# A decoder trunk on one core: the attention weight's piece emitted behind the step's Strassen operand

## The chip, the cores and the metric

The kernel runs on one core of one Trainium2 chip. The metric is the device time of one execution in microseconds; the time of a kernel is the median of several runs. Three runs of the kernel before are at hand, and one further execution was taken with the profiler.

## The reference

The reference is a trunk of two layers over 512 tokens of width 1024, in float32. Layer 0 mixes by causal pooling, layer 1 by stick-breaking attention with 16 heads of 64. Each layer ends in a squared-ReLU MLP of inner width 4096. The shared key and value projection stands between the layers.

```python
def sq_relu_mlp(h, w_up, w_down):
    u = jnp.matmul(h, w_up)
    return jnp.matmul(jnp.square(jax.nn.relu(u)), w_down)

def reference(x, ...):
    for layer in range(DEPTH):
        h = rms_norm(x, mix_pre_g[layer])
        m = pool_mixer(...) if layer < N_A else (stick_breaking_attention(q, k, v) @ w_o)
        x = x + rms_norm(m, mix_post_g[layer])
        h = rms_norm(x, mlp_pre_g[layer])
        x = x + rms_norm(sq_relu_mlp(h, w_up[layer], w_down[layer]), mlp_post_g[layer])
        if layer == N_A - 1:
            kv = jnp.matmul(rms_norm(x, kv_norm_g), w_kv)
    return x
```

## The kernel before

**Numbers in two parts.** Every matrix product is made of float32 values that are split into a high part, rounded to the fast matmul type (fp32r), and a low part, the difference. One product then takes three matmuls: high by high, high by low, low by high. A split is a copy on ScalarE and a subtraction on VectorE: L192 and L194 for the weights that are loaded raw and split at once (`weight`), L314 and L315 for everything that `split` handles.

**The first MLP** (`mlp` with l = 0) has 32 blocks of the up projection, 128 inner columns each, named by j. An up block is 24 matmuls (`up_block`, L766 to L770). ScalarE then takes ReLU and square (L675, L676). The down projection of the first 28 blocks is done in five groups of 2, 3, 3, 3 and 3 pairs of blocks, each by Strassen's scheme (the class `Seven`): seven products in place of eight, each with an operand `a` made of squares (`left`, additions on VectorE at L595) and an operand `w` made of down weights (`right`, L614). Both are split. `make(i)` makes the operands of product i; `product` (L640) runs its matmuls, 18 for a group of three pairs, and adds two halves of the result to y (L649, in part L646). The raw down weights come in two large loads a group, `load(0)` and `load(1)` (L579), in the tiles w1 and xn3. The last four blocks, 28 to 31, are not done by Strassen: their four down weights (dn28 to dn31) are loaded and split at the end of the stage, and `finish` runs their matmuls (L333 to L335).

**One step** of the stage is product i of group g. In code it is: the product, then the call that splits a piece of an attention weight, then the next up block, then the operands of product i + 2 (of the next group at the end of a group), then `fill`, which asks for the next weight in the queue. Steps count from 0 to 34 over the five groups; steps 1 to 33 have a piece.

**Pieces.** Thirty attention weights of 128 x 1024 (key, query, value and output) are prepared during this stage, so that attention need not split them: `split_apart` at L230. Each passes through four calls in a row: it is loaded (L245) into one of five buffers (three with the tag "apart", the spare tile, the tile of the gain row); it is scaled on ScalarE, column group by column group (L204; eight instructions for a key or query, four for a value, none for an output weight); its high part is copied into one half of the tile wx (L254) and the low part is made in place (L255); both parts are stored to device memory (L235, tensors "kept"). Every call does one of these for each of up to four pieces. Later, `make` at L265 brings the two parts back as they are ("w<-kept"). The first piece is loaded in step 1, the last in step 30 and stored in step 33.

**What orders the work.** Outside the stages that name a manual order, the order of each engine's instructions is worked out at build time by a scheduler with modelled durations (`schedule_with_timeline_sim=True`); where several instructions are ready, the one emitted first goes first. `tc.issue_after(x)` ties what is emitted within it to run behind x on x's engine. Around `split_apart` stand two of them, with the last split on ScalarE and on VectorE (`latest`). The weight copies of the up blocks are tied in the same way to `behind`, which is brought up to `latest` ahead of each fill. DMAs all go out on SyncE's queue in one order.

**Buffers at the end of the stage.** Tiles with the same tag share buffers, and a new tile waits for the last use of the old one. In step 33 the code takes tiles for the four down weights out of buffers that the stage no longer needs: dn30's raw weight and its high part get two of the three "apart" buffers, those of the last pieces but two and but one; dn31's raw weight gets a buffer of the Strassen operand a, that of product 5 of the last group. The fourth value weight that attention wants (v03 here) comes back into the tile wx, which the high parts of the pieces used. In the queue of weights, the four first value weights stand ahead of the four down weights.

Of the kernel before, what the change touches and what calls it, by code (L numbers as in the profile page):

```python
# [36 lines left out]
def halves(x, n=1):  # L37
    return x.rearrange("p (h a b) -> p h a b", h=n, a=2)


def unwoven(x, n=1):
    return x.rearrange("p (h b a) -> p h a b", h=n, a=2)
# [83 lines left out]
def trunk(ctx, tc, x, bands, grow, pw, wup, wdn, wq, wk, wv, wo, out):  # L126
# [12 lines left out]
    def name(s):  # L139
        uid[0] += 1  # L140
        return f"{s}{uid[0]}"

    def ps():
        return psum.tile([P, 512], F32, tag="ps", name=name("ps"))
# [19 lines left out]
    def spare_tile():  # L164
        return work.tile([P, D], F32, tag="spare", name=name("spare"))
# [10 lines left out]
    behind, latest = {}, {}  # L176
# [53 lines left out]
    def split_apart(mp):  # L230
        if going and going[0] is not None and going[0][1] == 3:
            k, _, raw, hi, _ = going.pop(0)
            kept[k] = dram.tile([2, P, D], F32, tag=f"kept{len(kept)}", name=name("kept"))
            for n, t in enumerate((hi.bitcast(F32), raw)):
                latest["sp"] = nc.sync.dma_start(kept[k][n], t)  # L235
        if apart:
            k, src, scaled = apart.pop(0)
            n = len(apart) % 5
            if n < 3:
                raw = mp.tile([P, D], F32, tag="apart", bufs=3, name=name("apart"))  # L240
            else:
                raw = spare_tile() if n == 3 else work.tile([P, D], F32, tag="grow", name=name("apart"))

            with tc.issue_after(latest["sp"].ins) if "sp" in latest else nullcontext():
                nc.sync.dma_start(raw, src)  # L245
            going.append([k, 0, raw, None, scaled])
        for x in going:
            k, n, raw, hi, scaled = x
            if n == 1:
                if scaled is not None:  # L250
                    scaled(raw)
            elif n == 2:
                hi = x[3] = apart_hi[0][:, len(kept) % 2]
                nc.scalar.copy(hi, raw)  # L254
                nc.vector.tensor_tensor(out=raw, in0=raw, in1=hi.bitcast(F32), op=ALU.subtract)  # L255
            x[1] += 1
# [19 lines left out]
    def get(key):  # L276
        while key not in made:
            make()
        return made.pop(key)
# [265 lines left out]
    def y_tiles():  # L545
        return [work.tile([P, D], F32, tag=f"y{t}", name=name(f"y{t}")) for t in range(T)]
# [104 lines left out]
    def mlp(l, mp, update):  # L651

        gate[0] = False
        y = y_tiles()
        firsts = [2 * sum(GROUPS[:g]) for g in range(len(GROUPS))]
        plain = 2 * sum(GROUPS)
        groups = [Seven(l, firsts[g], n, mp) for g, n in enumerate(GROUPS)]

        steps = [n for n in range(1, 34)] if l == 0 else []
        squares = []  # L660
        written = {None}

        def up(j, pu=None):
            if pu is None:
                pu = ps()
                up_block(pu, get(("up", l, j)), slice(0, S))
                n = 1
            else:
                n = 2
            if j < plain:  # L670
                g = max(g for g, f in enumerate(firsts) if f <= j)
                r = groups[g].part(j - firsts[g])
            else:
                r = mp.tile([P, S], F32, tag="rp", name=name("rp"))
            nc.scalar.activation(halves(r, n), unwoven(pu, n), ACT.Relu)  # L675
            nc.scalar.activation(r, r, ACT.Square)  # L676
            if j >= plain:
                if j < plain + 3:
                    if j == plain:
                        squares.append(mp.tile([P, 3, 2, S], F32R, tag="r", bufs=2, name=name("sq")))  # L680
                    a = squares[0][:, j - plain]
                else:
                    a = work.tile([P, 2, S], F32R, tag="spare", name=name("sq"))
                split(r, a[:, 0], a[:, 1])
                squares.append((a[:, 0], a[:, 1]))

        entering = dict(normed_by)
        groups[0].load(0)
        groups[0].squares()
        if l == 0:  # L690
            apart_hi[0] = wts.tile([P, 2, D], F32R, tag="wx", name=name("wx"))
        need(0, 1)
        n0 = 2 * GROUPS[0]
        first = early[:]
        while len(first) < n0:
            first.append((ps(), get(("up", l, len(first)))))
        for j, (pu, w) in enumerate(first):
            if j == n0 - 1:
                need(2, 3)
                groups[0].load(1)  # L700
            if j >= len(early):
                up_block(pu, w, slice(0, S // 2))
        early.clear()
        for j, (pu, w) in enumerate(first):
            up_block(pu, w, slice(S // 2, S))
            up(j, pu)
            fill()

        with tc.issue_after(latest["act"].ins), tc.issue_after(latest["dve"].ins):
            for i in range(2):  # L710
                groups[0].make(i)
        for g, group in enumerate(groups):
            coming = groups[g + 1] if g + 1 < len(groups) else None
            if coming:
                coming.squares()
            ups = list(range(firsts[g + 1], firsts[g + 1] + 2 * GROUPS[g + 1]) if coming else range(plain, NJ))
            if g == 0:
                up(ups.pop(0))
                fill()
            else:  # L720
                with tc.issue_after(latest["dve"].ins):
                    while entering:
                        entering.popitem()[1].homogeneous_eps()
            for i in range(7):
                group.product(i, y, written if g == 0 else None)
                if 7 * g + i in steps:
                    with tc.issue_after(latest["act"].ins), tc.issue_after(latest["dve"].ins):
                        split_apart(mp)
                if ups:
                    up(ups.pop(0))  # L730
                if i + 2 < 7:
                    group.make(i + 2)
                    if i + 2 == 4 and coming:
                        coming.load(0)
                    if i + 2 == 6 and coming:
                        coming.load(1)
                elif coming:
                    coming.make(i + 2 - 7)
                elif i == 5:
                    piece = lambda tag, k, bufs=1: mp.tile([P, k, D], F32R, tag=tag, bufs=bufs, name=name("dn"))  # L740
                    w, e, x = piece("w1", 3), piece("e", 1), piece("w", 3, 2)
                    c = piece("apart", 1, 3)[:, 0]
                    dn_raw["dn", l, NJ - 2] = mp.tile([P, D], F32, tag="apart", bufs=3, name=name("dn"))
                    dn_raw["dn", l, NJ - 1] = mp.tile([P, D], F32, tag="a", bufs=2, name=name("dn"))
                    dn_pool[0] = [[w[:, 0], w[:, 1]], [w[:, 2], e[:, 0]], [c, x[:, 2]], [x[:, 0], x[:, 1]]]

                if l == 0:
                    behind.update(latest)
                fill(1 + (coming is None and i == 6))
        assert not apart and not going  # L750
        gpost = gain_row((R_MLP_POST0, R_MLP_POST1)[l])
        count[0] = 0
        w = [get(("dn", l, j)) for j in range(plain, NJ)]
        dn_pool[0] = None
        fill(ahead)
        finish(l, squares[1:], w, y, lambda t, y: update(t, y, gpost))
# [21 lines left out]
    with tc.tile_pool(name="mix0", bufs=1, reuse_waits="tile") as mp:  # L778
# [138 lines left out]
        def half_up(j):  # L917
# [3 lines left out]
        steps = {  # L921
            "j": lambda n: nc.gpsimd.tensor_copy(eye, wpool[n][:, D:]),
            "z": busy, "r": scale_row, "e": scale_copy, "w": linear, "q": first_squares, "v": first_norm,
            "b": own_band, "p": pooled, "c": copied, "f": reached, "m": mixed,
            "s": lambda t, h: ups[t].squares_of(h, left["m", t, h]),
            "g": lambda t, h: ups[t].product(h, left["m", t, h]),
            "X": lambda t: (ups[t].first_total(nc.vector), ups[t].first_rstd()),
            "Y": lambda t: (ups[t].second_total(nc.vector), ups[t].rstd()),
            "V": lambda t: ups[t].first_rstd(), "a": lambda t, h: ups[t].add_part(h),
# [490 lines left out]
```

## Time and profile before

| | |
|---|---|
| median of 3 runs | 905.44 us (904.74 to 905.92) |
| profiled execution | 904.5 us |
| its span, first to last instruction | 902.7 us |
| granted TensorE clock, mean | 0.999 |
| bytes moved by DMA | 155.73 MB |
| the first MLP's steps in the trace | about 60 to 324 us |

The profile names engines PE (TensorE's matmuls), PEld (its weight loads, beside them), DVE (VectorE), ACT (ScalarE), POOL (GpSimd) and SP (SyncE, whose queue issues the DMAs: SPq). "out<-in" are the program's tile names with the buffer numbers left out; L254 is line 254 of the kernel before. A row of a timeline has start, length, engine, line, operation, tiles, shapes and a count; in brackets stands the idle time ahead of it and what ended that. The length of an issue row is the time to issue; the time to landing comes from the view of the DMAs. In the chain of waits each row is a start, a length and what the end of the program waited for at that time.

### The profile page before, as it was taken

The page shows a single profiled execution, that of the slowest core. Times are in us where ns is not written, and L with a number is a line of the kernel's source. Part 1 is how long each engine was busy: PE and PEld are TensorE (multiplying, and loading weights), DVE is VectorE, ACT ScalarE, POOL GpSimd, SP SyncE. Part 2 cuts the span into 40 slices and gives each one's busy share as a digit, 9 for nine tenths or more (in the row PEclk, how much of TensorE's full clock was granted, in tenths as well). Part 3 has the DMA queues.
Part 4 walks back from the last instruction along what each step waited for, and adds up shares of the span by engine and source line. Part 5 has one row for each costly group of instructions (what it writes and reads, how often), then busy time and mean ns, then how long its engine had stood idle before and what let it go on. Part 6 is the DMA issues. An engine that isn't in the chain of part 4 may idle for free.

```text
span 902.7 us, 12343 instructions
## 1 busy us (share of the span) xinstructions
PE 890.8 (99%) x4688; PEld 786.0 (87%) x4688; DVE 692.7 (77%) x797; ACT 557.3 (62%) x986; POOL 40.9 (5%) x85
## 2 busy tenths in 40 slices
PE   9999999999999999999999999999999999999997
PEld 7998888888888878888999888898888888888886
DVE  5876798998978977268777489885696976957866
ACT  6668979888784747256555474875545454544632
POOL 3200000000000004000000001200000000000002
PEclk9999999999999999999999999999999999999999
DMA  8444969789697770643152371342504233133002
GB/s 306 142 147 150 358 219 367 305 277 401 223 343 263 269 273 2 216 157 140 57 189 82 109 288 47 141 163 77 203 26 162 94 140 117 47 140 117 23 24 94
DMA packets 42973, 155.73 MB, mean 173 GB/s; under 512 B 4257, under 2 KB 4385, under 8 KB 42914
## 3 DMA queue, kind: packets, MB, share of 16 engines
q1 hardware_dynamic: 42914, 154.95, 47.8%
q8 instruction: 37, 0.61, 0.3%
q14 instruction: 22, 0.18, 0.1%
HBM read 121.38 MB, written 33.55 MB: 172 GB/s over the span
## 4 chain that ended last, share of the span: by engine, by line
PE 84%; DVE 5%; DMA 4%; ACT 4%; issue 2%; POOL 1%; SPq 0%; POOLq 0%; ACTq 0%; DVEq 0%
PE ps L640 24%; PE ps L769 14%; PE ps L766 14%; PE ps L770 14%; PE ps L334 4%; PE ps L335 4%; PE ps L333 4%; PE ps L1105 2%; PE ps L1124 2%; PE ps L1149 2%; DMA xn<-in_wdn 1%; PE ps L440 1%; DMA apart<-in_wk 1%; PE ps L894 1%; ACT xn L318 1%
## 5 line engine op out<-in xcount | busy, mean ns | idle before, releaser
L640 PE MATMUL ps<-w,a 128*128 128x512 f32 x1176 | 265.9, 379 | 0.4 <-ACT a L314 0.4
L769 PE MATMUL ps<-xnh,w 128*128 128x512 f32 (+1 forms) x704 | 253.4, 362 | 0.0
L770 PE MATMUL ps<-xnl,w 128*128 128x512 f32 (+1 forms) x704 | 252.8, 360 | 0.0
L766 PE MATMUL ps<-xnh,w 128*128 128x512 f32 (+1 forms) x704 | 252.3, 360 | 0.3 <-DVE w L915 0.3
L640 PEld LDWEIGHTS ps<-w,a 128*128 128x128 f32 x1176 | 222.0, 189 | 32.7 <-ACT a L314 0.8
L766 PEld LDWEIGHTS ps<-xnh,w 128*128 128x128 f32 x704 | 132.9, 190 | 16.0 <-DVE w L915 0.4
L770 PEld LDWEIGHTS ps<-xnl,w 128*128 128x128 f32 x704 | 133.5, 190 | 15.2
L769 PEld LDWEIGHTS ps<-xnh,w 128*128 128x128 f32 x704 | 133.0, 190 | 15.4
L194 DVE TENSOR_TENSOR w<-raw,w 128x1024 fp32r<-128x1024 f32 x58 | 70.8, 1221 | 46.9 <-ACT w L192 46.9
L649 DVE TENSOR_TENSOR y<-ps,y 128x512 f32<-128x512 f32 x124 | 84.0, 686 | 25.7 <-PE ps L640 25.2
L192 ACT CAST w<-raw 128x1024 fp32r<-128x1024 f32 x58 | 60.6, 1045 | 64.1 <-PE ps L766 62.6
L314 ACT CAST a<-r 128x768 fp32r<-128x768 f32 (+1 forms) x60 | 47.4, 789 | 62.3 <-PE ps L640 40.9
L315 DVE TENSOR_TENSOR a<-r,a 128x768 fp32r<-128x768 f32 (+1 forms) x60 | 54.0, 899 | 10.8 <-ACT a L314 10.8
L314 ACT CAST w<-e 128x1536 fp32r<-128x1536 f32 (+1 forms) x30 | 41.7, 1391 | 32.1 <-DVE e L614 23.9
L1086 DVE TENSOR_TENSOR_SCAN e<-u,begin 128x1280 f32<-128x1280 f32 x16 | 45.2, 2825 | 18.6 <-ACT u L1070 17.9
L315 DVE TENSOR_TENSOR w<-e,w 128x1536 fp32r<-128x1536 f32 (+1 forms) x30 | 49.4, 1646 | 0.7 <-ACT w L314 0.5
L204 ACT ACTIVATE apart<-apart,eye 128x128 f32<-128x128 f32 (+1 forms) x132 | 43.0, 404 | 0.2 <-DMA apart<-in_wk 0.2
L315 DVE TENSOR_TENSOR w<-xn,w 128x1536 fp32r<-128x1536 f32 (+1 forms) x20 | 33.0, 1649 | 4.5 <-ACT w L314 4.1
L675 ACT ACTIVATE r<-ps 128x512 f32<-128x512 f32 x56 | 33.0, 589 | 5.4 <-PE ps L766 5.4
L676 ACT ACTIVATE r<-r 128x512 f32<-128x512 f32 x56 | 35.3, 631 | 1.3
L315 DVE TENSOR_TENSOR w<-w,w 128x1536 fp32r<-128x1536 f32 (+1 forms) x20 | 33.0, 1648 | 3.5 <-ACT w L314 3.5
L322 POOL TENSOR_SCALAR stat<-stat,eps 128x1 f32<-128x1 f32 x8 | 5.4, 680 | 604.9 <-ACT xn L318 604.9
(140 smaller groups left out, 1322.1 us busy)
## 6 DMA issues: line engine op xcount, KB each, us to landing
raw<-in_wup SPq DMA_DIRECT2D x64, 512.0 KB, 4.5
w<-kept SPq DMA_DIRECT2D x60, 512.0 KB, 4.3
kept<-wx SPq DMA_DIRECT2D x30, 512.0 KB, 5.6
w<-in_wdn SPq DMA_DIRECT2D x8, 1536.0 KB, 7.0
kept<-apart SPq DMA_DIRECT2D x24, 512.0 KB, 6.2
xn<-in_wdn SPq DMA_DIRECT2D x8, 1536.0 KB, 8.2
apart<-in_wk SPq DMA_DIRECT2D x7, 512.0 KB, 8.0
apart<-in_wq SPq DMA_DIRECT2D x7, 512.0 KB, 9.6
```

Of the source, the lines that this page charges most:

```text
L192: nc.scalar.copy(hi, raw)
L194: nc.vector.tensor_tensor(out=lo, in0=raw, in1=hi.bitcast(F32), op=ALU.subtract)
L204: nc.scalar.mul(c, c, gc[:, at : at + 1])
L314: latest["act"] = nc.scalar.copy(hi, src)
L315: latest["dve"] = nc.vector.tensor_tensor(out=lo, in0=src, in1=hi.bitcast(F32), op=ALU.subtract)
L333: nc.tensor.matmul(dst, ah, bh, start=start, stop=False)
L640: nc.tensor.matmul(bank, a[:, x, q, TS[t]], woven(w[:, z, q], NS[0]), start=start and q == 0 and k == 0, stop=q == self.n - 1 and k == 2, ...
L649: nc.vector.tensor_tensor(out=part, in0=bank, in1=part, op=ALU.add)
L766: nc.tensor.matmul(pu[:, cols], wl[:, k, :], moving(xnh, k), start=False, stop=k == KC - 1)
L769: nc.tensor.matmul(pu[:, cols], wh[:, k, :], moving(xnh, k), start=k == 0, stop=False)
L770: nc.tensor.matmul(pu[:, cols], wh[:, k, :], moving(xnl, k), start=False, stop=False)
L1086: nc.vector.tensor_tensor_scan(out=self.e[:, ::-1], data0=self.u[:, 1:][:, ::-1], data1=begin[:, ::-1], initial=0.0, op0=ALU.mult, op1=ALU ...
```

## The change

The call of `split_apart`, with its two `issue_after`, moves within the step: from ahead of the step's up block and operands to behind them. It stands ahead of `behind.update(latest)` and `fill` as before. What a call does is unchanged, and so are the steps that have one. As `latest` now holds the splits of the step's own operands, the piece's instructions on ScalarE and VectorE are tied to run behind those; before they were tied behind the operands of the step before. In step 33 the call comes behind the lines that take the tiles for the down weights.

```diff
             for i in range(7):
                 group.product(i, y, written if g == 0 else None)
-                if 7 * g + i in steps:
-                    with tc.issue_after(latest["act"].ins), tc.issue_after(latest["dve"].ins):
-                        split_apart(mp)
                 if ups:
                     up(ups.pop(0))
                 if i + 2 < 7:
                     group.make(i + 2)
...
                     dn_pool[0] = [[w[:, 0], w[:, 1]], [w[:, 2], e[:, 0]], [c, x[:, 2]], [x[:, 0], x[:, 1]]]
 
+                if 7 * g + i in steps:
+                    with tc.issue_after(latest["act"].ins), tc.issue_after(latest["dve"].ins):
+                        split_apart(mp)
                 if l == 0:
                     behind.update(latest)
                 fill(1 + (coming is None and i == 6))
```

## The prediction

> **What bounds the kernel now.** First the page's head and its busy lines.
>
> ```profile
> span 902.7 us, 12343 instructions
> PE 890.8 (99%) x4688; PEld 786.0 (87%) x4688; DVE 692.7 (77%) x797; ACT 557.3 (62%) x986; POOL 40.9 (5%) x85
> ```
>
> TensorE is busy in 99% of the span. What matters is how much of the missing 1% lies where the change acts. The waits of TensorE alone answer that; the columns are total us, times, longest.
>
> ```profile
> PE ps L334 <- DVE dn L194: 0.8, 1, 0.8
> PE ps L333 <- ACT dn L192: 0.5, 1, 0.5
> PE ps L640 <- ACT a L314: 0.4, 1, 0.4
> ```
>
> These three are all that TensorE waits in the first MLP. Cut into stretches, the stage looks like this (columns: length, then busy us of PE, PEld, DVE, ACT, POOL, the granted clock, DMA share, GB/s):
>
> ```profile
> 109.00:172.00 63.00, 63.00 (x293) 55.02 (x292) 58.62 (x66) 53.74 (x98) 0.00 (x0) 1.00 0.83 308
> 172.00:230.00 58.00, 57.56 (x268) 50.21 (x267) 54.08 (x53) 49.81 (x88) 0.00 (x0) 1.00 0.81 300
> 324.50:349.00 24.50, 23.25 (x110) 19.68 (x109) 17.52 (x24) 12.24 (x29) 5.99 (x10) 1.00 0.33 120
> ```
>
> The second row is short of its length by 0.44 us (the L640 wait, near 172 us), the third by 1.25 us (the two dn waits). So the stage can give back 0.44 + 1.25 = 1.69 us and no more, which is 0.19% of 905.44. The clock is 1.00 throughout. The first row shows where a loss could come from: VectorE is busy 58.62 of 63 us, with 4.4 us of slack.
>
> Is a busy TensorE at its pace? In the chain, one step of a three-pair group runs from one product to the next:
>
> ```profile
> 307.63 3.88 PE ps L640 x18
> 316.69 7.78 PE ps L640 x36
> ```
>
> The 18 matmuls of the first line and the 24 of the up block behind it take 316.69 - 307.63 = 9.06 us, 0.216 us each, and 18 x 0.216 = 3.88 fits the same pace. The change alters no matmul, so this pace stays.
>
> **What the change moves.** Each piece passes through four calls, one a step: load, scaling (L204), high part and subtraction (L254, L255), two stores. In code the call moves behind the up block and the operands of the same step. Where does it stand on ScalarE now? At the start and at the end of the stage:
>
> ```profile
> 80.04 1.04 ACT L314 CAST w<-w 128x1024 fp32r<-128x1024 f32 x1
> 80.98 1.05 ACT L254 CAST wx<-apart 128x1024 fp32r<-128x1024 f32 x1
> ...
> 312.29 1.47 ACT L314 CAST w<-xn 128x1536 fp32r<-128x1536 f32 x1
> 313.66 1.04 ACT L254 CAST wx<-apart 128x1024 fp32r<-128x1024 f32 x1
> ...
> 321.35 1.47 ACT L314 CAST w<-xn 128x1536 fp32r<-128x1536 f32 x1
> 322.72 1.99 ACT L192 CAST dn<-raw 128x1024 fp32r<-128x1024 f32 x2
> ```
>
> The operand w<-w at 80.04 is product 4's, made in step 2; the first L254 belongs to step 3's call (load in 1, scale in 2, split in 3). The last L254 belongs to step 32 and stands behind product 5's operand, made in step 31. So each piece already runs right behind an operand split, that of the step before, because ScalarE has nothing else while the up block runs. issue_after ties it now to the last split of the step before; afterwards to this step's own. The whole chain of pieces thus slides by one step, about 9.06 us, and nearly every slot behind an operand stays filled, by the piece one earlier.
>
> **Middle steps.** Two rows price a piece, eight scalings on ScalarE and a subtraction on VectorE:
>
> ```profile
> 105.40 2.44 ACT L204 ACTIVATE apart<-apart,eye 128x128 f32<-128x128 f32 x8
> ...
> L255 DVE TENSOR_TENSOR apart<-apart,wx 128x1024 f32<-128x1024 f32 x24 | 29.2, 1218 | 0.6 <-ACT wx L254 0.6
> ```
>
> Same instructions, same places behind operands: 0 us. What can still differ is the turn between a piece and the weight copy L192 of the same step, since a piece is now emitted ahead of that step's fill. That puts up to 1.05 + 2.44 us of ScalarE (L254 and eight L204) ahead of a copy whose block is two steps of 9 us away: covered. If that cover fails at the one place where an operand was late, the bound is one piece's subtraction (L255) more, against the whole wait less: between -0.44 and +1.22 us. I take 0, because the work per step is unchanged. [...] DMA order with the big wdn loads also stays: the store of a piece is already issued when its split is done, not when its call is emitted.
>
> **The end of the stage.** Here one step later is not neutral, because the four down weights come next. The chain of waits there:
>
> ```profile
> 324.49 7.14 DMA dn<-in_wdn
> 331.73 1.05 ACT dn L192
> 332.81 1.24 DVE dn L194
> 334.09 0.48 PE ps L334
> ```
>
> The last raw weight (dn31) takes the buffer of product 5's operand a, so its load starts when that product ends, at 324.49. It lands 7.14 us later, and split it ends TensorE's 1.25 us wait. The SyncE queue around it, then the time to landing of three of these transfers:
>
> ```profile
> 312.22 0.49 SPq L235 DMA_DIRECT2D kept<-apart  x1
> 314.73 0.32 SPq L235 DMA_DIRECT2D kept<-wx  x1
> 316.72 0.88 SPq L265 DMA_DIRECT2D w<-kept  x2
> 321.95 0.80 SPq L265 DMA_DIRECT2D w<-kept  x2
> 322.80 0.43 SPq L235 DMA_DIRECT2D kept<-apart  x1
> 324.49 0.33 SPq L182 DMA_DIRECT2D dn<-in_wdn  x1
> ...
> kept<-apart SPq DMA_DIRECT2D x1, 512.0 KB, 8.5
> ...
> kept<-wx SPq DMA_DIRECT2D x1, 512.0 KB, 7.1
> ...
> dn<-in_wdn SPq DMA_DIRECT2D x1, 512.0 KB, 3.7
> ```
>
> The pair at 321.95 brings the fourth value weight (v03) back. It goes into the wx buffer, so it waits for the last kept<-wx: 314.73 + 7.1 = 321.8. It is in flight when dn31 is issued, and so is the last kept<-apart.
>
> VectorE's rows for the last pieces and for dn30:
>
> ```profile
> 316.28 1.22 DVE L255 TENSOR_TENSOR apart<-apart,wx 128x1024 f32<-128x1024 f32 x1
> ...
> 323.16 1.75 DVE L315 TENSOR_TENSOR w<-xn,w 128x1536 fp32r<-128x1536 f32 x1
> ...
> 327.70 1.22 DVE L194 TENSOR_TENSOR dn<-dn,dn 128x1024 fp32r<-128x1024 f32 x1
> ```
>
> After the change the last L254 comes behind product 6's split, at 322.72, and ends near 323.8; the last kept<-wx goes out then. Its landing, 323.8 + 7.1 = 330.9, releases v03's loads. They fall behind dn31 instead of ahead of it. The last subtraction follows the split's own, which ends at 324.9, so the raw store goes out near 326.1. Of three transfers of 0.5 MB issued in the 2.5 us ahead of dn31, one is left. Two fewer are 1.05 MB, at the rate of that stretch
>
> ```profile
> 327.00:331.70 4.70, 4.70 (x23) 4.12 (x22) 2.52 (x3) 0.00 (x0) 0.00 (x0) 1.00 1.03 416
> ```
>
> an estimated 2.5 us. dn31 would land after 4.6 us, between the 3.7 of its sister and the 7.14, and the wait of 1.25 us would go.
>
> What is late next is the third down weight (dn30). Its raw goes into a buffer of the pieces, freed by the store of piece 28 of 30, and its high part into the buffer of piece 29. Piece 28's store moves to the place of piece 29's (312.22, landing after 8.5): 320.7. A load of 3.7 to 7.1 us ends at 324.4 to 327.8, and with 1.05 and 1.24 us of split it is ready at 326.7 to 330.1. TensorE wants its low part here:
>
> ```profile
> 329.82 0.38 PE L334 MATMUL ps<-dn,sq 128*128 128x512 f32 x1
> ```
>
> So 0 to 0.3 us late; if instead piece 29's store, going out between 317.5 (the end of the subtraction at 316.28) and 320.7, takes 8.5 us, the high part starts at 329.2 and the low part ends at 331.6, 1.8 us late. A wait there replaces dn31's rather than adds to it, as 12 matmuls (2.6 us) lie between the two. The subtraction of the last piece also pushes the splits of dn28 to dn30 on VectorE by 1.2 us, and dn30's now ends at 327.70 + 1.22 = 328.92, 0.9 us ahead of the row above: 0.3 us late again.
>
> The end's wait is thus 0 to 1.8 us in place of 1.25: -1.25 to +0.55. I take 0.85 left, -0.4, as dn30's row is nearer to in time than late. v03 itself, landing near 338, is not wanted before the projection that begins here:
>
> ```profile
> 352.57 0.38 PE L333 MATMUL ps<-w,xnh 128*128 128x512 f32 x1
> ```
>
> **Sum.** 0 - 0.4 = -0.4 us. The profiled execution took 904.5 us, 902.7 of span and 1.8 around it: 904.1. That execution lies 0.9 under the median of the runs, 905.44, so against that 905.0. Bounds of the terms: -1.69 to +1.77, 903.7 to 907.2.
>
> **Rivals.** (a) *Slower: SyncE stands still ahead of dn31.* SyncE takes its queue in order, and v03 already held it from 317.6 to 321.95 with a finished store behind. If dn31's load is queued behind the raw store of the last piece it starts at about 326.1, +1.6 us; if behind v03's loads, at 330.9, +6.4 us, giving 906.1 or 910.9 on the profile's scale (907.0 and 911.8 against the median). It decides at one point: whether the last kept<-wx lands before product 5 ends. 323.8 against 324.49 leaves no time for a transfer of 7.1, so the schedule, which is made with modelled durations, should put dn31 first: 0.10.
>
> (b) *Both waits go.* 1.69 us less, 902.8 on the profile's scale, 903.8 against the median. It needs dn30 in time and VectorE's order near 172 to turn out better: 0.10.
>
> (c) *Nothing moves.* If pieces stayed behind the operands that they follow now, the time is 905.4. issue_after forbids it for all but the last calls: 0.10.
>
> (d) *VectorE's tight stretch breaks.* The schedule of the stage is worked out anew, and TensorE's own order with it. One or two operands late by one subtraction each: +1.2 to +2.4, so 906.7 to 907.9. For it: 58.62 of 63 us busy, and one wait of 0.44 there already. Against: an unchanged load per step. 0.08.
>
> [...]
>
> **How the numbers follow.** The forecast, a shift by one step and an end that is worth a few tenths, gets 0.60; its own range is 903.8 to 906.0. What a measurement of this kernel can tell from no change is about 0.2%, 1.81 us. The forecast and (c) lie inside it; of (b) 0.04 may be measured as faster, with (e) 0.06. Of (a) the longer hold, 0.07, and of (d) 0.05 are slower: 0.12. That leaves 0.82 for no change. The range 903.5 to 907.4 takes in the bounds of the terms, (b), (c) and the lesser halves of (a) and (d).
>
> **What would show it.** Right: the first L254 near 88 behind w<-xn, the last near 322.7 behind the last w<-xn; w<-kept of v03 issued near 331, after dn<-in_wdn at about 324.5; dn<-in_wdn landing in 4 to 6 us; the dn waits of TensorE at 0 to 1 us; rows of the middle stretches as before. Wrong: an L254 still at 313.7; dn<-in_wdn issued after 326; TensorE waits at L640 of over 1 us between 100 and 300; a span below 901 without any change in the three waits.

## The result and the profile after

The kernel after took 908.69 us (906.21 to 912.30, 14 runs) beside 904.46 for the kernel before on the same chip (14 runs): a ratio of 1.0047, 95% interval 1.0036 to 1.0058. It is slower by 4.2 us, more than twice what the prediction called no change. Its profiled execution took 907.5 us, with 905.7 of span, 3.0 more than before.

The shift by one step is there as forecast. First ScalarE at the end of the stage, then SyncE's queue with the issue rows of the same stretch:

```profile
321.88 1.47 ACT L314 CAST w<-xn 128x1536 fp32r<-128x1536 f32 x1
323.26 1.04 ACT L254 CAST wx<-apart 128x1024 fp32r<-128x1024 f32 x1
```

```profile
312.14 0.32 SPq L235 DMA_DIRECT2D kept<-apart  x1
318.29 0.33 SPq L182 DMA_DIRECT2D dn<-in_wdn  x1
318.72 0.38 SPq L235 DMA_DIRECT2D kept<-wx  x1
319.19 1.80 SPq L265 DMA_DIRECT2D w<-kept  x2
321.09 0.67 SPq L235 DMA_DIRECT2D kept<-apart  x1
...
325.02 0.62 SPq L182 DMA_DIRECT2D dn<-in_wdn  x1
...
331.38 0.80 SPq L265 DMA_DIRECT2D w<-kept  x2
```

The last L254 stands behind the last operand (forecast 322.7), and v03's pair goes out at 331.38, behind dn31's load at 325.02 (forecast 331 and 324.5). The time went elsewhere. TensorE's waits in the stage, and the two rows at the end (the bracket is the idle time ahead of the row):

```profile
PE ps L333 <- ACT dn L192: 1.2, 1, 1.2
PE ps L640 <- ACT a L314: 1.2, 1, 1.2
PE ps L334 <- DVE dn L194: 0.8, 1, 0.8
```

```profile
331.53 0.48 PE L333 MATMUL ps<-dn,sq 128*128 128x512 f32 x1 [1.22 <-ACT dn L192]
332.79 0.48 PE L334 MATMUL ps<-dn,sq 128*128 128x512 f32 x1 [0.78 <-DVE dn L194]
...
334.14 0.63 PE L333 MATMUL ps<-dn,sq 128*128 128x512 f32 x1
334.57 0.63 PE L334 MATMUL ps<-dn,sq 128*128 128x512 f32 x1
335.00 0.63 PE L335 MATMUL ps<-dn,sq 128*128 128x512 f32 x1
```

The dn waits are 2.00 us, and they now belong to dn30, one block earlier than the dn31 waits of before. Behind them the matmuls start 0.43 us apart instead of 0.216. The stretches say why; the third column from the right is the granted clock:

```profile
324.50:349.00 24.50, 22.50 (x97) 18.62 (x96) 17.98 (x24) 11.33 (x24) 3.71 (x6) 0.93 0.51 191
...
334.00:335.00 1.00, 1.00 (x4) 0.72 (x4) 1.00 (x1) 0.00 (x0) 0.00 (x0) 0.50 1.06 414
335.00:336.00 1.00, 1.00 (x4) 0.81 (x3) 0.07 (x1) 0.00 (x0) 0.00 (x0) 0.50 0.95 311
336.00:338.00 2.00, 2.00 (x8) 1.64 (x7) 0.19 (x1) 0.00 (x0) 0.00 (x0) 0.70 0.93 354
```

From 333.8 to 337.2 the clock is 0.50: eight matmuls at 0.43 instead of 0.216 us, 1.7 us that no busy share shows, since TensorE has 3.42 of 3.42 us busy there.

The L640 wait stands where the second group ends and the third begins. VectorE there, before and then after:

```profile
162.60 0.68 DVE L649 TENSOR_TENSOR y<-ps,y 128x512 f32<-128x512 f32 x1
163.20 1.75 DVE L614 TENSOR_TENSOR e<-xn,w 128x1536 f32<-128x1536 f32 x1
...
170.80 0.95 DVE L595 TENSOR_TENSOR r<-r 128x768 f32<-128x768 f32 x1
171.67 1.22 DVE L255 TENSOR_TENSOR spare<-spare,wx 128x1024 f32<-128x1024 f32 x1
```

```profile
161.12 1.76 DVE L614 TENSOR_TENSOR e<-xn,w 128x1536 f32<-128x1536 f32 x1 [2.03 <-DMA xn<-in_wdn]
...
170.20 1.22 DVE L255 TENSOR_TENSOR apart<-apart,wx 128x1024 f32<-128x1024 f32 x1
171.34 0.95 DVE L595 TENSOR_TENSOR r<-r 128x768 f32<-128x768 f32 x1
```

Among what changed places in the newly planned order are these two instructions. (TensorE's own order of up blocks and products changed too, in places between 135 and 245 us.) The combine e<-xn, for the operand w of the third group's second product, moved ahead of the low part of an operand (a<-r) and of an addition to y, and now waits 2.03 us for its 1.5 MB load, with both behind it. The piece's subtraction moved ahead of r<-r, for the operand a of the same product, the one that TensorE waits for.

The books of the two executions: start of the program 0.25 us earlier, L640 wait 1.22 against 0.44 (+0.78), dn waits 2.00 against 1.25 (+0.75), clock +1.7: together +3.0, the span's difference. This execution lies 1.2 us under its kernel's median; the waits differ from run to run, and so does the clock. Nine of the 14 runs of after have a mean granted clock of 0.997 or less, against 14 of the 93 runs of before that were timed beside the experiments. The five runs of after with 0.999 took 906.2 to 909.2 us, so the clock is only a part of the loss.

### The profile page after: what moved, and what is told of

It is laid out like the page before. It is cut to its first block, busy times and chain, and to the rows that moved or that the text cites. A ratio compares the mean times of both kernels' runs of the same rounds, so it can differ in the third digit from the quotient of the medians.

```text
span 905.7 us, 12335 instructions
## 1 busy us (share of the span) xinstructions
PE 892.5 (99%) x4688; PEld 787.2 (87%) x4688; DVE 693.4 (77%) x797; ACT 557.3 (62%) x986; POOL 41.4 (5%) x85
## 4 chain that ended last, share of the span: by engine, by line
PE 83%; DVE 6%; ACT 4%; DMA 3%; issue 2%; POOL 1%; SPq 0%; POOLq 0%; ACTq 0%; DVEq 0%
PE ps L640 23%; PE ps L769 14%; PE ps L766 14%; PE ps L770 14%; PE ps L334 4%; PE ps L335 4%; PE ps L333 4%; PE ps L1105 2%; PE ps L1124 2%; PE ps L1149 2%; DMA kept<-apart 1%; PE ps L440 1%; PE ps L894 1%; DMA xn<-in_wdn 1%; DMA kept<-wx 1%
## 5 line engine op out<-in xcount | busy, mean ns | idle before, releaser
L640 PE MATMUL ps<-w,a 128*128 128x512 f32 x1176 | 265.8, 379 | 1.2 <-ACT a L314 1.2
L640 PEld LDWEIGHTS ps<-w,a 128*128 128x128 f32 x1176 | 222.0, 189 | 33.2 <-ACT a L314 1.6
```

The lines of the kernel that those rows point to most:

```text
L640: nc.tensor.matmul(bank, a[:, x, q, TS[t]], woven(w[:, z, q], NS[0]), start=start and q == 0 and k == 0, stop=q == self.n - 1 and k == 2, ...
```

## The experiments

Each was timed beside runs of the kernel before on the same chip; "before" is that batch's median. In kernels with added lines, numbers in rows are up to four higher (L643 is the L640 of above, L337 is L334).

**Middle alone and end alone.** The call at its new place in groups 0 to 3 and at its old one in group 4, then the reverse:

```diff
+                if 7 * g + i in steps and g == 4:   # second kernel: g < 4
+                    with tc.issue_after(latest["act"].ins), tc.issue_after(latest["dve"].ins):
+                        split_apart(mp)
...
-                if 7 * g + i in steps:
+                if 7 * g + i in steps and g < 4:    # second kernel: g == 4
```

> The piece is emitted behind the operands in groups 0 to 3 and ahead of the up block, as before, in group 4. The middle is that of the changed kernel, the end that of the kernel before. Theory 'end' (the late store of the last piece but one holds back dn30's high part, TensorE idles and its clock falls): the 330 us stretch is that of before, waits of about 1.25 us, clock 1.00; time 905.3, which is 904.5 plus the 0.8 us that the middle lost. Rival 'middle' (VectorE's new order in the tight stretch is what costs): about 908.7, as the changed kernel.

> The reverse: ahead of the up block in groups 0 to 3, behind the operands in group 4 alone. Theory 'end': TensorE waits about 2 us for dn30 near 331 and is granted 0.5 of its clock for some 3 us behind it; time 907.5 to 908.5. Rival 'middle': 904.5, as before.

The middle alone: 906.74 us beside 904.61, ratio 1.0027 (1.0009 to 1.0044). The end alone: 904.70, ratio 1.0003 (0.9992 to 1.0015). The first lies between the two theories; the second is what theory 'middle' had. So about half of the loss is the middle by itself, and the end by itself costs nothing in the median. A rest, 2.0 us by the medians and 1.5 by the ratios, seems to appear only with both, but the intervals are too wide to show that. In the profiled execution of the middle alone (909.0 us, over its median) the combine waits 3.28 us and TensorE 2.46:

```profile
162.74 1.76 DVE L614 TENSOR_TENSOR e<-xn,w 128x1536 f32<-128x1536 f32 x1 [3.28 <-DMA xn<-in_wdn]
```

```profile
174.83 1.13 PE L640 MATMUL ps<-w,a 128*128 128x512 f32 x4 [2.46 <-ACT a L314]
```

Neither profiled execution is typical of its kernel at the end of the stage. The middle alone has the old end there, but dn waits of 1.16 and 0.78 us with a clock of 0.50 behind them. The end alone took 906.9 us, 2.2 over its median, and shows just what theory 'end' named: waits of 1.44 and 0.78 us and 3.4 us at 0.50. Two of its 12 runs have a mean clock of 0.997 or less, so the loss at the end comes in some runs and not in most.

**dn30's high part in another buffer.** Here dn30's high part goes into a buffer that is free early, so that it need not wait for piece 29's raw store; then, in the kernel before, dn30's high part and dn31's raw weight were given later buffers:

```diff
-                    c = piece("apart", 1, 3)[:, 0]
+                    c = piece("r", 2, 2)[:, 0]
```

```diff
-                    c = piece("apart", 1, 3)[:, 0]
                     dn_raw["dn", l, NJ - 2] = mp.tile([P, D], F32, tag="apart", bufs=3, name=name("dn"))
-                    dn_raw["dn", l, NJ - 1] = mp.tile([P, D], F32, tag="a", bufs=2, name=name("dn"))
+                    dn_raw["dn", l, NJ - 1] = mp.tile([P, D], F32, tag="apart", bufs=3, name=name("dn"))
+                    c = piece("apart", 1, 3)[:, 0]
```

> The changed kernel with one edit: dn30's high part goes into the buffer of the squares r of the last group, which its last operand has freed near 323, and not into a buffer of the pieces. Theory 'end': dn30 is split by about 328, its wait goes; dn31 (load near 325, 7.5 us to land, 2.3 us of split) is then the one that ends the wait, some 1.5 to 2 us, as TensorE is earlier by that much. Time 906 to 907.5, depending on whether the clock still falls. Rival 'middle': 908.7. Rival 'clock' (the clock falls for another reason than the wait): 0.93 in the stretch 324.5 to 349 as in the changed kernel, with dn30's wait gone.

> The kernel before, pieces where they were, with one edit: dn30's high part takes the buffer of the last piece, dn31's raw weight that of the last but one. dn31 comes earlier and dn30's high part waits for the last store, about 322.8 + 7.6 = 330.4, as in the changed kernel. Theory 'end': TensorE waits about 2 us at dn30 and the clock falls to 0.5 behind it; 906 to 907.5. Rival 'middle': 904.5 or less, as only the wait changes places. Rival 'clock': a wait of 2 us, but 1.00 throughout, 905.2.

The first took 910.49 us, ratio 1.0061 (1.0039 to 1.0084): no cure. dn30's wait is gone, but dn31's load, issued at 326.08, lands only at 336.6, and its waits are 3.39 and 0.78 us. So freeing this buffer alone does not help; that something common holds up dn30 and dn31 is what this suggests, and the swap below tests it. The second took 909.22, ratio 1.0050 (1.0033 to 1.0067). It gave dn31 the buffer that is stored last, its load went out at 331.52, and its profile shows waits of 0.94 and 0.77 us. With 1.25 us in before, they are 0.5 of the 3.3 us by which this execution is late against that of before. The other 2.8 us were lost by 22 us, ahead of anything that the edit moves: TensorE waits 2.25 us for `own` (L866; 0.82 in before), and behind that the clock is 0.50 for 3.4 us (its mean over the first 60.7 us is 0.97, 1.00 in before). Why the median of 11 runs is 4.6 us higher stays open, and the kernel tells nothing of dn30.

**dn28 and dn29 first.** TensorE's written order of the last products was changed so that dn30 is wanted 2.6 us later, in the kernel after and in the kernel before:

```diff
-    last_steps("""p00012 p01012 p003 v00 s00 p013 v01 s01 g00 g01 V0 p100123 v10 s10 a00 S00 a01 S01 g10 W0
-    p110123 v11 s11 g11 V1 n00 n01 p200123 v20 s20 a10 S10 a11 S11 g20 W1 p210123 v21 s21 g21 V2 n10 n11
+    last_steps("""p0001 p0101 p1001 p1101 p0023 v00 s00 p0123 v01 s01 g00 g01 V0 p1023 v10 s10 a00 S00 a01 S01 g10 W0
+    p1123 v11 s11 g11 V1 n00 n01 p200123 v20 s20 a10 S10 a11 S11 g20 W1 p210123 v21 s21 g21 V2 n10 n11
```

> The kernel after, with TensorE's hand-written order of the last products of the stage changed: the 24 matmuls of dn28 and dn29 (8 + 16) all run first, and those of dn30 behind them, so dn30 is wanted 2.6 us later and dn31 some 3.5 us later. No piece, load or split moves. Theory E (the end costs through the late down weights: waits of 1.22 + 0.78 us and then eight matmuls at half the clock, 1.7 us): both waits go, the clock stays at 1.00 in 324.5 to 349, and the kernel comes to 908.7 - 2.0 - 1.7 = 905 us, or 906.5 if about 1.5 us of the middle (the L640 wait of 1.2) and of a lower mean clock stay. Theory M (the end is the same in both kernels and all of the loss lies in the middle, at the boundary of the second and third group): it falls by no more than the end's waits of before, 1.25 us, to 907.5 or above. Theory C (the mean clock falls with the even load, not with waits): no change beyond the waits, 907.

> The kernel before with the same order of the last products: dn28 and dn29 first. In its profile the two dn waits are 1.25 us together, and no drop of the clock follows them. Theory E: the waits go, 904.5 - 1.25 = 903.2 us. In runs in which the wait is longer than in the profile, the drop of the clock goes too, so the runs lie closer together. A rival: the order moves the wait to another down weight, or to a PSUM buffer that is not free; then 904.5 as before.

In the kernel after: 907.77 us, ratio 1.0032 (1.0017 to 1.0046). The clock holds and dn30 is in time, but waits of 0.4 and 0.8 us are still there. They are dn31's now, whose load took 9.4 us to land. Theory E's 905 missed. The kernel before with this order took 905.95, ratio 1.0009 (0.9996 to 1.0022): the dn waits are gone from its profile, and it is not faster. In its profile the order has put a new wait behind the stage, where TensorE transposes the next normed tokens:

```profile
349.12 1.05 PE L440 MATMUL ps<-eye,xn 128*128 128x128 f32 x6 [1.07 <-ACT xn L430]
```

A wait of the same length (L440, 1.1 us) stands in the kernel after with this order, and in neither kernel without it (0.7). So the order itself takes back most of the 1.25 us. Another 0.6 us of this execution (L866 1.18 against 0.82, L640 0.65 against 0.44) lie ahead of it.

**The piece behind the left operand.** `lact` and `ldve` are the last splits of the left operand:

```diff
-            self.operands[i] = self.left(i), self.right(i)
+            a = self.left(i); latest["lact"], latest["ldve"] = latest["act"], latest["dve"]
+            self.operands[i] = a, self.right(i)
...
-                    with tc.issue_after(latest["act"].ins), tc.issue_after(latest["dve"].ins):
+                    with tc.issue_after(latest["act"].ins), tc.issue_after(latest["dve"].ins), tc.issue_after(latest["lact"].ins), tc.issue_after(latest["ldve"].ins):
```

> The kernel after, with each piece's split tied also behind the split of the left operand of the same step (not only the right). At the boundary of the second and third group the piece's subtraction (1.22 us) then stands behind the operand's addition L595, as in the kernel before, instead of ahead of it; the weight's combine (e<-xn), which waits for its load, still stands ahead of both. Theory S (the subtraction ahead of the operand costs its own length): the L640 wait of 1.22 falls to 0.4 or less, and the kernel comes to about 907.5. Theory X (the wait comes from the combine that stands exposed to the landing of its load, 2 us): the wait stays near 1.2, and the time at 908.7; in executions where the load lands later the wait is 2 us and more as in the first experiment's 2.5. The end is as in the kernel after: both waits and the drop of the clock.

905.57 us, ratio 1.0012 (0.9993 to 1.0031), better than either theory had it. The newly planned order differs from that of after in many places, TensorE's order among them. Two matter here: the subtraction is behind r<-r, and at the end the store kept<-wx of piece 29 stands ahead of dn30's load (315.22 and 317.50), where the kernel after has it behind (318.72 and 318.29). Its dn waits are 0.1 us. At the boundary:

```profile
161.90 1.76 DVE L614 TENSOR_TENSOR e<-xn,w 128x1536 f32<-128x1536 f32 x1 [1.29 <-DMA xn<-in_wdn]
```

```profile
173.17 1.13 PE L641 MATMUL ps<-w,a 128*128 128x512 f32 x4 [0.52 <-ACT a L314]
```

How do the two theories of the middle stand? In six executions with e<-xn exposed, its wait and TensorE's are 1.29 and 0.52 (this one), 1.85 and 1.41 (the swap below), 2.03 and 1.22 (after), 2.06 and 1.23 (after with dn28 and dn29 first), 2.35 and 1.52 (high part in another buffer), 3.28 and 2.46 (middle alone). TensorE waits 0.8 us less in five of them and 0.4 in one. In all six VectorE has no idle time from e<-xn to r<-r, so what the load is late by reaches TensorE. That bears out theory X. It does not rule out theory S: in the same unbroken row the subtraction ahead of r<-r adds its length, and this kernel is no test of that, since two additions to y stand in its place:

```profile
170.11 1.28 DVE L650 TENSOR_TENSOR y<-ps,y 128x512 f32<-128x512 f32 x2
171.31 0.94 DVE L595 TENSOR_TENSOR r<-r 128x768 f32<-128x768 f32 x1
```

Nor is the wait zero in the order of before, where no load is exposed: 0 (end alone), 0.44 (before), 0.49, 0.65 (before with the two edits above) and 1.21 us (end alone with the swap, below). The mean of these five is 0.56, that of the five executions with the order of after 1.57.

**The combine behind the operand.** In the third group e<-xn is tied behind the subtraction of the first left operand; the piece's subtraction comes behind r<-r with it:

```diff
-                combine(e, w22, w12)
+                with tc.issue_after(latest["adve"].ins) if (self.l, self.first) == (0, 10) else nullcontext(): combine(e, w22, w12)
...
-            self.operands[i] = self.left(i), self.right(i)
+            if i == 0: a = self.left(i); latest["adve"] = latest["dve"]
+            self.operands[i] = (a if i == 0 else self.left(i)), self.right(i)
```

> The kernel after, with VectorE's order at that boundary put back as in the kernel before: the combine e<-xn of the third group's weight is tied behind the first subtraction of the group's first left operand, and the piece's subtraction stands behind the operand's addition. Theory X+S: the L640 wait falls to 0.4 us or less whatever the landing of xn (up to 2 us of it are covered), and the kernel comes to 908.7 - 2.2 = 906.5 us (2.2 is what the first experiment, the middle alone, lost against before), leaving the end's loss. Against it, theory C (the middle's loss is lower clock or DMA, not VectorE's order): the wait goes and the time stays within 0.7 us of 908.

906.59 us (906.5 was expected), ratio 1.0016 (0.9999 to 1.0034): 2.1 us less than after by the medians. The wait near 173 us is gone. That the number is met to 0.1 us is in part luck, for the profiled execution is made up otherwise. Another wait of 1.29 us stands at 164.71, where ScalarE had waited for a piece's load that took 11.19 us to land; the order that was put back is not proof against that. And the end, with its rows in the order of after, cost less here: dn waits of 0.58 and 0.78 us with 3 us of work between them, and no fall of the clock. Nor is the order that of before: r<-r now stands ahead of the low part of w<-e, and on TensorE five matmuls of the up block stand ahead of the product that waited. So this run shows that planning this place anew gives the time back, and not which of these moves does it.

**One swap in SyncE's queue.** dn30's load is tied behind piece 29's kept<-wx; by the traces that is the only change of order against the kernel after on any engine:

```diff
+                if n == 0:
+                    wxs.append(latest["sp"])
...
-        nc.sync.dma_start(raw, src)
+        with tc.issue_after(wxs[28].ins) if first else nullcontext():
+            nc.sync.dma_start(raw, src)
...
-        made[k] = weight(src, place(k), scaled, dn_raw.pop(k, None))
+        made[k] = weight(src, place(k), scaled, dn_raw.pop(k, None), k == ("dn", 0, NJ - 2))
```

> The kernel after with one swap in SyncE's queue and no other instruction moved on any engine: dn30's load is tied behind the store of piece 29's high part. In the kernel after it stands ahead of that store, waits 3 us for piece 28's raw store to land, and holds behind it the high part's store, the pair of v02 and the raw store of piece 29, whose landing dn30's high part waits for. Theory Q (the end's loss is this queue): the high part's store goes out near 315.3 instead of 318.7, the raw store of piece 29 near 319 instead of 321.1, the dn30 waits of 1.2 + 0.8 us go to 0.8 or less, the clock holds 1.00, and the time falls by what the end added on top of the middle, 2 us: 906.7. Theory R (dn30's raw or dn31 is late as well, only hidden): the waits move to dn31 and the time stays above 908.

905.66 us beside 904.30, ratio 1.0024 (1.0014 to 1.0034): 3.0 us less than after by the medians and 2.1 by the ratios, from one issue moved by one place. The queue, and ScalarE's split of dn30:

```profile
312.20 0.32 SPq L236 DMA_DIRECT2D kept<-apart  x1
315.28 0.32 SPq L236 DMA_DIRECT2D kept<-wx  x1
319.74 0.33 SPq L183 DMA_DIRECT2D dn<-in_wdn  x1
320.17 0.86 SPq L268 DMA_DIRECT2D w<-kept  x2
321.11 0.38 SPq L236 DMA_DIRECT2D kept<-apart  x1
```

```profile
328.98 1.05 ACT L193 CAST dn<-dn 128x1024 fp32r<-128x1024 f32 x1 [2.76 <-DMA kept<-apart]
```

The store of 0.5 MB that was ready at 315.2 now goes out then, 3.4 us earlier. Part of the expectation missed: piece 29's raw store still goes out at 321.11, because dn30's load waits for piece 28's store as before. But the store ahead of it is 3.4 us further on its way, and it lands in 7.8 us instead of 9.2. The waits are 0.8 for dn30 and 0.8 for dn31, 1.6 in all with 3 us of work between them, and the clock stays at 1.00:

```profile
324.50:349.00 24.50, 22.95 (x109) 19.25 (x108) 19.30 (x25) 12.89 (x28) 5.23 (x9) 1.00 0.51 191
```

**The same swap with the end alone.** The diff above, in the second experiment's kernel:

> The second experiment (pieces of groups 0 to 3 at the old place, of group 4 at the new) with the same swap in SyncE's queue. Theory Q: the middle is that of before, with its wait of 0.44, and the dn waits fall from 1.25 in before, and 2.2 in the profile of the second experiment, to 0.5 or less: 904.5 - 0.9 = 903.6 us, below both kernels. Theory R: dn31 becomes the wait in its place, as in before, and the time is 904.5.

903.37 us beside 904.30, ratio 0.9991 (0.9980 to 1.0001). It is the best of the study, with dn waits of 0.2 us in its profile, but its interval touches 1: a gain of a tenth of a per cent is likely, not shown. The expected wait of 0.44 at L640 was 1.21 in its profile, though VectorE and TensorE have the order of before there and e<-xn does not wait.

**Less on the DMA engines.** Two pieces' loads became memsets, which leaves two attention weights at zero:

```diff
-                nc.sync.dma_start(raw, src)
+                if len(going_n) in (10, 11):
+                    nc.gpsimd.memset(raw, 0.0)
+                else:
+                    nc.sync.dma_start(raw, src)
+                going_n.append(0)
```

> The kernel after, but the raw loads of two pieces (those issued at 146.05 and 152.88 us, 0.5 MB each) are left out and replaced by a GpSimd memset of the buffer; these two attention weights are then zero, and the order of the boundary of the second and third group on VectorE is that of the kernel after, the piece's subtraction still ahead of the operand's addition L595. Theory X (the wait there comes from the combine e<-xn exposed to its load, in a stretch where the DMA rate stands at 417 GB/s): 1.05 MB less is 2.5 us, xn lands that much earlier, the wait of 2.0 us in front of e<-xn goes, and with it the L640 wait; the time falls by 1.2 to 2 us, to 907. Theory S (only the subtraction's place counts): L640 waits 1.2 us as before and the time stays at 908.7.

909.21 us, ratio 1.0063 (1.0044 to 1.0081): a miss. The xn load, issued at 153.70, still lands after 9.7 us, and the DMA rate from 150 to 165 is still 415 to 420 GB/s, so 1 MB less did not shorten what was queued. What sets the 9.7 us stays open. The waits did fall in the profile, e<-xn's to 0.64 us and TensorE's at the boundary to 0.43, in an order that was planned anew. The profiled execution, 2.9 us over the median, lost its time elsewhere: 1.5 us by 22 us, 1.0 of it a longer wait of TensorE for `own` (1.60 against 0.62), and 2.4 at the end, with dn waits of 2.84 and 0.47 and 6.8 us at a clock of 0.50.

**Both orders put back.** The swap and the combine's tie in one kernel, with every piece at its new place. (Its expectation's "seventh run" is the kernel with the combine tied.)

> The kernel after with two orders put back and every piece at its new place: the swap in SyncE's queue at the end, and the combine e<-xn of the third group behind the operand's subtraction on VectorE, as in the seventh run. If the loss is these two orders, both cures together give back 2.0 + 2.1 us: 904.6, the time of before. If the shift by a step costs anything by itself (a lower clock, another load on the DMA engines), it stays above 906.

903.52 us beside 904.30, ratio 0.9996 (0.9983 to 1.0009), where 904.6 was expected. TensorE has no L640 wait, and 0.11 us is all that it is idle at the end:

```profile
172.00:230.00 58.00, 58.00 (x270) 50.79 (x269) 54.37 (x53) 49.26 (x88) 0.00 (x0) 1.00 0.81 299
324.50:349.00 24.50, 24.39 (x120) 20.74 (x120) 19.59 (x27) 14.00 (x30) 5.98 (x10) 1.00 0.46 179
```

By ratios the combine's tie gives back 0.0031 and the swap 0.0023 of the 0.0047; together 0.0051. So with these two places changed, nothing is left of the loss that the interval can show (its upper end is 0.0009, or 0.8 us), though every piece stands one step later. Two reservations stay. The cures do more than put orders back, as the kernel before has waits of 1.69 us in these stretches and this one none. And the first cure carries the other moves named above.

## Why the prediction was wrong

**What bounds the kernel** held: TensorE at 0.216 us a matmul, 1.69 us to win at most. "The clock is 1.00 throughout" held for before, and "The change alters no matmul, so this pace stays" carried it over to after without a reason. It failed there: eight matmuls at 0.43 us, 1.7 us in the profiled execution.

**The shift by one step** held in the rows that were named for it.

**Middle steps, "Same instructions, same places behind operands: 0 us"** is the first step that failed. It argued from the pieces' own places; what moved were other instructions around them, when the order of VectorE was planned anew. It measured +2.1 us by the medians (the middle alone, or what the combine's tie gives back) against bounds of -0.44 to +1.22. The upper bound was one subtraction's length. The wait for a load, 2.03 us on VectorE in the profile, had no term in the sum. Rival (d) named this place, this cause (the order planned anew) and +1.2 to +2.4, and had 0.08: "an unchanged load per step" is no argument about an order. Its price, by late subtractions, was right in size; how much of the loss is the subtraction and how much the load is not shown.

**The end.** dn31's load did fall ahead of v03's, but dn31 did not land in 4.6 us: 7.5 in the profile after. That dn30 is late next was right, and so was the named worst case, 1.8 us through piece 29's store (2.00 measured; its own terms add up to 331.5 and 1.7). Taking 0.85 from that range was the wrong choice: the store "between 317.5 and 320.7" went out at 321.09 and landed after 9.2 us instead of 8.5, because dn30's load stood in SyncE's queue waiting for piece 28's store, with a ready store and the pair of v02 behind it. That is rival (a)'s mechanism, one load earlier than where it was looked for. The prediction named that load's landing but not its place among SyncE's rows.

**The sum** missed on both terms, +0.78 and +0.75 in the profile instead of 0 and -0.4, and on the missing third, the clock, +1.7. Rivals (b) and (c) did not come. The 0.02 that (e) adds to the chances is for a term that no run shows, time left on a busy TensorE: from 109 to 172 us TensorE was busy 63.00 of 63 us before and 62.99 after, and the fastest of all runs, one with both orders put back, took 902.49 us.

## What to carry to other kernels

Where a scheduler plans the order, a moved call is priced by what else may be planned around it: look for instructions whose input is a load that lands just in time (here e<-xn), and ask what stands behind them on their engine if they come first. A profiled execution can lie 2 us off its kernel's median, so ask of each whether its waits are the usual ones. In SyncE's queue a load that waited for a buffer was a wall for the finished store behind it (dn30's load out at 318.29, the store ready at 315.2 out at 318.72); one issue put behind one store was worth two to three us of 909. Read the granted clock beside every wait that grows.

## What was not expected of the hardware

Short waits can cost twice. Idle times of 1.22 and 0.78 us, 0.5 us of work between them, were followed by 3.4 us at a clock of 0.50, 1.7 us more. The same came after 1.16 + 0.78 (middle alone), 1.44 + 0.78 (end alone), 3.39 + 0.78 (high part in another buffer), 2.84 + 0.47 (two loads less, for 6.8 us) and one wait of 2.25 us near the start of the program (dn30's high part late, in the kernel before). It did not come after 0.47 + 0.78 (before), 0.94 + 0.77, two times 0.78 with 3 us of work between them (the swap), nor, and this is the odd one, after the single 2.46 us at 172.4 in the middle alone. So the sum of the idle time does not decide it.

The traces of before and after list when the granted clock changed. In after it stands at 1.00 from 6.12 us on, falls to 0.50 at 333.80, is back at 337.21 and falls again at 903.83; in before it stands at 1.00 from 5.80 on and falls at 900.09. Counted from the first of these times, the changes come after 327.68, 331.09 and 897.71 us in after and after 894.29 in before, that is 96, 97, 263 and 262 times 3.4133 us. Counted in such lengths, after has 1.92 of the 2.00 us of its dn waits in the one that ends at 333.80, where the clock falls. No other holds more than 1.22 us in after and 0.82 in before, the program's last 10 us left out, and none of them ends in a fall. How much idle time it takes, these two traces do not show.

A load of 0.5 MB at the end of the stage is hard to time: dn31's took 7.14 us before, 7.5 after, 3.5 with dn30's high part late and 10.5 with it in another buffer.
